# Loaded operand tiles are rounded later in the instruction lists of a one-core encoder layer

## The chip, the core and the metric

The kernel runs on one core of a Trainium2 chip. The metric is the device time of one execution in microseconds (us). Five engines work beside each other, each through its own list of instructions in order: PE multiplies matrices, DVE and ACT work on vectors, POOL does a little, and SP issues almost all transfers (DMA). An instruction that waits for another engine or for a transfer holds all that stands behind it in its list.

## What is computed

One layer of a hybrid encoder on a sequence of 2048 tokens of width 1024, all in float32:

```
xn = rms_norm(x)
[aq|ak|av|mq|mk|mv|mo|i|f|ga|gm] = xn @ w_in
A = chunked band attention (8 heads of 64; own chunk of 64 and 8 before; relative bias)
M = mLSTM matrix memory (4 heads of 128), conv on q and k, norm, sigmoid gate
y = sigmoid(ga) * (A @ w_att_proj) + sigmoid(gm) * (M @ w_mlstm_proj)
x = x + y @ w_out
x = x + relu(rms_norm(x) @ w_up)^2 @ w_down
out = rms_norm(x)
```

## The kernel before

Tokens are in four blocks of 512, two blocks to a half `s`. Large products are made with seven block products in place of eight, on sums and differences of operands; `m` numbers the seven. Each float32 operand is split into two rounded parts, a high part and the rest, and a product takes three matmuls (`mm3`, L562 to L564, and the loop of L631 and L662). A weight tile `wsp` is split by a cast on ACT (L501) and a subtract on DVE (L503). There are three `wsp` buffers, so the next split waits until PE is done with an older tile.

The other operand is kept in one of 28 tiles `r`, each of two parts. Some operands are made in one stage, stored in DRAM in float32, and loaded later into such a tile, into its second part. `take_u1` (L2101) does that: SP issues the load (L2103), `split` (L1106) casts the tile's second part to its first part on ACT (L1109), and DVE subtracts in place (L1114). It serves three sources: `xu`, the input's combinations for the later input projection (`take_batch`, 28 tiles); `u`, the hidden layer of the feed-forward part (`take_u`, 224 tiles, in a ring of 8 tiles for the first half and 16 for the second); and `mix`, pieces of the attention and memory results (`load_mix`). The down product (`down`, L806) goes through `m` and four chunks `c`, takes four `u` tiles for each, and gives them back to the ring. During the first half's down product PE also does attention and memory work for blocks 2 and 3; during the later input projection it does that for blocks 0 and 1.

The order of the instructions is found by a planner, `Flow`, when the program is built. Each step is a Python generator that yields its engine, the time that it is reckoned to keep the engine, and, for a load, the further time until it has landed. `Flow.run` always takes the step that can start first by these times, and writes its instructions down. These times are no waits: on the chip, only semaphores make an engine wait. They decide where an instruction stands in its engine's list. The tool that builds the program may move instructions a little after that; an instruction on DVE is bound not to pass one that the planner puts over 10 us earlier, on ACT over 6 us earlier.

Names that recur: L1674 adds parts of the memory's result on DVE; L1262 is the product of attention weights and values on PE; L1273 copies a bank on ACT and L1275 adds on DVE behind it; L1116 and L1765 on DVE prepare the operand `y`.

Of the kernel before, what the change touches and what calls it, by code (L numbers as in the profile page):

```python
# [101 lines left out]
class Flow:  # L102
# [12 lines left out]
               sp=dict())  # L115
# [130 lines left out]


class Layer:
    LATE = 4000.0

    def __init__(self, tc, pool, psum, io):
        self.tc, self.nc, self.io = tc, tc.nc, io
# [197 lines left out]
    def split_w(self, i, src, raw, sent=None):  # L450
        if i == 0:
            yield from self.split_first(src, raw, sent)
            self.fl.put(self.wraw, raw, late=self.LATE)
            return
# [4 lines left out]
        yield from self.split_now(i, raw)  # L459
        self.fl.put(self.wraw, raw, late=self.LATE)  # L460

    def split_turned(self, i, srcs, raw):
# [3 lines left out]
        yield from self.split_now(i, raw)  # L466
        self.fl.put(self.wraw, raw, late=self.LATE)

# [38 lines left out]
    def quad_w(self, i, q, kept, raws, evs):  # L507
# [10 lines left out]
        def sub(n, dst, x, y):  # L518
            yield "dve", dve_ns(1024)
            V.tensor_sub(dst, x, y)  # L520
            if kept:
                fl.spawn(keep(n, dst), 1)
            else:
                fl.set(spilt[n])
# [16 lines left out]
        yield from sub(2, b, d, b)  # L541
        fl.put(self.wraw, d, late=self.LATE)
        yield "wait", [spilt[1]]
        yield from sub(3, a, c, a)
        fl.put(self.wraw, c, late=self.LATE)
        yield from self.split_now(i + 5, b)
        yield "wait", [spilt[2]]
        fl.put(self.wraw, b, late=self.LATE)
        yield from self.split_now(i + 6, a)
# [1549 lines left out]
        fl.put(self.rpool, *(yield "get", ring, N_RING[s]))  # L2099

    def take_u1(self, src, r, ev):  # L2101
        yield "sp", 800, 2000
        self.nc.sync.dma_start(r[:, 1].bitcast(F32), src)  # L2103
        yield from self.split(r[:, 1].bitcast(F32), r)
        self.fl.set(ev)
# [458 lines left out]
```

## Time and profile before

| | before |
|---|---|
| median of 3 runs | 2750.84 us (2749.84 to 2754.76) |
| profiled execution | 2753.07 us, span 2751.3 us |
| PE busy | 2724.6 us (99%) |
| DVE busy | 2086.0 us (76%) |
| ACT busy | 1526.4 us (55%) |
| HBM | 458.79 MB read, 212.21 MB written |

The page gives busy time as a share of the span, and for groups of instructions their count, busy time, mean time of one, and the idle time of the engine just before them with what ended it. A matmul's row gives 390 ns, but matmuls overlap, so their spacing is less. All times are counted from the span's start.

### The profile page before, as it was taken

Reading aid. Unit: us, or ns where it says so; the run is one execution under the profiler, and the core shown is the slowest. Engines: PE = TensorE matmul, PEld = TensorE weight load, DVE = VectorE, ACT = ScalarE, POOL = GpSimd, SP = SyncE. Lnnn points to the kernel's source line nnn. Section 1 sums busy time; section 2 is a strip of 40 time slices with the busy share of each in tenths; the row PEclk is TensorE's granted clock in tenths of the full one; section 3 lists DMA queues with packets and bytes.
Section 4 is the critical chain, followed back from the end, with each engine's and each line's share of the span. In section 5 each row is a group of like instructions: output and inputs, shape, how many; then the busy total and the mean of one; then the engine's idle time right before and its main releaser. Section 6 shows DMA issues by size and latency. Waiting matters only on the chain.

```text
span 2751.3 us, 38074 instructions
## 1 busy us (share of the span) xinstructions
PE 2724.6 (99%) x12832; PEld 2261.5 (82%) x12832; DVE 2086.0 (76%) x3689; ACT 1526.4 (55%) x2640; POOL 44.6 (2%) x79
## 2 busy tenths in 40 slices
PE   9999999999999999999999999999999999999998
PEld 8878888788888887888888888888888888888887
DVE  7878776888775778897768889888888665667675
ACT  6545446666652434566556766657345565554443
POOL 0000000000000000000000000000000000000000
PEclk9999999999999999999999999999999999999999
DMA  8877678878877888767668778776864454588863
GB/s 295 284 254 268 234 267 281 260 235 266 255 256 254 299 305 294 244 212 260 246 237 295 254 231 223 239 257 199 294 227 171 151 205 154 180 278 281 283 230 137
DMA packets 331992, 673.57 MB, mean 245 GB/s; under 512 B 36900, under 2 KB 66468, under 8 KB 331796
## 3 DMA queue, kind: packets, MB, share of 16 engines
q1 hardware_dynamic: 331076, 670.08, 72.3%
q8 instruction: 101, 1.65, 0.2%
q10 hardware_dynamic: 720, 1.06, 0.1%
q14 instruction: 95, 0.78, 0.1%
HBM read 458.79 MB, written 212.21 MB: 244 GB/s over the span
## 4 chain that ended last, share of the span: by engine, by line
PE 83%; DVE 7%; DMA 4%; issue 3%; ACT 2%; POOL 0%; SPq 0%; POOLq 0%; DVEq 0%; ACTq 0%
PE bank L631 35%; PE bank L662 9%; PE bank L562 9%; PE bank L564 8%; PE bank L563 8%; PE bank L667 2%; PE bank L1337 2%; PE bank L1262 2%; PE bank L1369 2%; DVE wsp L503 1%; PE bank L856 1%; DVE r L1114 1%; DMA yp<-tmp 1%; DMA r<-u 1%; DVE ctx L1765 1%
## 5 line engine op out<-in xcount | busy, mean ns | idle before, releaser
L631 PE MATMUL bank<-r,wsp 128*128 128x512 f32 x4872 | 1110.9, 390 | 4.2 <-ACT r L1109 1.4
L631 PEld LDWEIGHTS bank<-r,wsp 128*128 128x128 f32 x4872 | 912.5, 188 | 198.2 <-ACT r L1109 2.1
L501 ACT CAST wsp<-wraw 128x1024 fp32r<-128x1024 f32 x439 | 461.3, 1051 | 492.1 <-PE bank L631 183.3
L503 DVE TENSOR_TENSOR wsp<-wraw,wsp 128x1024 fp32r<-128x1024 f32 x439 | 537.0, 1223 | 247.0 <-ACT wsp L501 236.7
L562 PE MATMUL bank<-r,wsp 128*128 128x512 f32 x1088 | 429.9, 396 | 0.3 <-DVE scs L1343 0.3
L564 PE MATMUL bank<-r,wsp 128*128 128x512 f32 x1088 | 425.3, 391 | 0.0
L563 PE MATMUL bank<-r,wsp 128*128 128x512 f32 x1088 | 425.2, 391 | 0.0
L662 PE MATMUL bank<-r,wsp 128*128 128x512 f32 x1512 | 370.8, 394 | 3.1 <-DVE ctx L780 2.5
L662 PEld LDWEIGHTS bank<-r,wsp 128*128 128x128 f32 x1512 | 279.4, 189 | 59.4 <-issue 2.7
L564 PEld LDWEIGHTS bank<-r,wsp 128*128 128x128 f32 x1088 | 204.3, 188 | 43.0
L562 PEld LDWEIGHTS bank<-r,wsp 128*128 128x128 f32 x1088 | 204.5, 188 | 38.4 <-DVE scs L1343 0.7
L563 PEld LDWEIGHTS bank<-r,wsp 128*128 128x128 f32 x1088 | 204.7, 188 | 38.1
L1114 DVE TENSOR_TENSOR r<-r 128x512 fp32r<-128x512 f32 x273 | 181.8, 687 | 56.8 <-ACT r L1109 55.0
L1109 ACT CAST r<-r 128x512 fp32r<-128x512 f32 x273 | 164.7, 621 | 104.4 <-DMA r<-u 77.1
L1798 DVE TENSOR_TENSOR ctx<-bank,ctx 128x512 f32<-128x512 f32 x150 | 103.0, 687 | 64.7 <-PE bank L631 63.6
L520 DVE TENSOR_TENSOR wraw<-wraw,wraw 128x1024 f32<-128x1024 f32 x112 | 136.5, 1220 | 2.2 <-DMA wsum<-wraw 1.0
L1350 ACT ACTIVATE sc<-sc,scs 128x640 f32<-128x640 f32 (+4 forms) x128 | 97.2, 760 | 54.9 <-DVE scs L1343 54.3
L1790 ACT COPY ctx<-bank 128x512 f32<-128x512 f32 x150 | 87.2, 581 | 52.0 <-PE bank L631 50.5
L2119 ACT ACTIVATE ctx<-ctx 128x512 f32<-128x512 f32 x96 | 60.5, 630 | 97.8 <-DVE ctx L1798 97.8
L1374 DVE TENSOR_TENSOR r<-bank,r 128x512 fp32r<-128x512 f32 (+1 forms) x168 | 96.4, 595 | 8.4 <-ACT r L1372 7.5
L1262 PE MATMUL bank<-r,r 128*128 128x512 f32 x336 | 95.7, 367 | 3.5 <-DVE ctx L1674 1.9
L1372 ACT CAST r<-bank 128x512 fp32r<-128x512 f32 (+1 forms) x168 | 80.7, 514 | 27.9 <-PE bank L1369 27.4
(257 smaller groups left out, 3054.1 us busy)
## 6 DMA issues: line engine op xcount, KB each, us to landing
wraw<-in_wf SPq DMA_DIRECT2D x196, 512.0 KB, 4.2
r<-u SPq DMA_DIRECT2D x224, 256.0 KB, 4.4
wraw<-wsum SPq DMA_DIRECT2D x104, 512.0 KB, 4.5
u<-ctx SPq DMA_DIRECT2D x128, 256.0 KB, 2.8
u<-tmp SPq DMA_DIRECT2D x96, 256.0 KB, 2.1
wraw<-in_w SPq DMA_DIRECT2D x47, 512.0 KB, 4.5
ctx<-in_wf SPq DMA_DIRECT2D x88, 256.0 KB, 4.2
wsum<-ctx SPq DMA_DIRECT2D x88, 256.0 KB, 3.1
```

The costliest lines, as they stand in the source:

```text
L501: nc.scalar.copy(w[:, 0], raw)
L503: nc.vector.tensor_sub(w[:, 1], raw, w[:, 0].bitcast(F32))
L520: V.tensor_sub(dst, x, y)
L562: mm(ps, lh, rh, start=first, stop=False)
L563: mm(ps, lh, rl, start=False, stop=False)
L564: mm(ps, ll, rh, start=False, stop=last)
L631: mm(ps, wv[:, x, k, n], a[:, y], start=new and k == 0 and x == y == 0, stop=k == 3 and x == 1, skip_group_check=True)
L662: mm(ps, wv[:, x, k, n], a[:, y], start=start and x == y == 0, stop=stop and x == 1, skip_group_check=True)
L1109: self.nc.scalar.copy(dst[:, 0], src)
L1114: self.nc.vector.tensor_sub(dst[:, 1], src, dst[:, 0].bitcast(F32))
L1262: nc.tensor.matmul(bkv[:, :, c0:c0 + w], st, sl[:, :, o:o + w], start=n == 0, stop=n == total - 1)
L1798: nc.vector.tensor_add(t[:, o:o + 512], ps, t[:, o:o + 512])
```

## The change

One number: the time after its issue at which the planner takes a tile loaded by `take_u1` as landed goes from 2000 to 10000 ns. The planner then lets the cast and the subtract start some 8 us later by its reckoning, and puts them further on in the lists of ACT and DVE. The load and the semaphores are as before. Where other steps fit in their place, the planner's later choices differ too.

```
 class Layer:
-    LATE = 4000.0
+    LATE, LANDED = 4000.0, 10000.0
...
     def take_u1(self, src, r, ev):
-        yield "sp", 800, 2000
+        yield "sp", 800, self.LANDED
         self.nc.sync.dma_start(r[:, 1].bitcast(F32), src)
         yield from self.split(r[:, 1].bitcast(F32), r)
         self.fl.set(ev)
```

More of the change, by code (lines that the diff above doesn't have):

```diff
@@ L248 @@
 class Layer:
-    LATE = 4000.0
+    LATE, LANDED = 4000.0, 10000.0
     def __init__(self, tc, pool, psum, io):
@@ L2101, in take_u1 @@
     def take_u1(self, src, r, ev):
-        yield "sp", 800, 2000
+        yield "sp", 800, self.LANDED
         self.nc.sync.dma_start(r[:, 1].bitcast(F32), src)
```

## The prediction

> **What bounds the kernel now.** I read the page first, for the busiest engine, then the waits of the moved line, then the windows and the chain of waits where that line holds somebody up.
>
> ```profile
> span 2751.3 us, 38074 instructions
> PE 2724.6 (99%) x12832; PEld 2261.5 (82%) x12832; DVE 2086.0 (76%) x3689; ACT 1526.4 (55%) x2640; POOL 44.6 (2%) x79
> L631 PE MATMUL bank<-r,wsp 128*128 128x512 f32 x4872 | 1110.9, 390 | 4.2 <-ACT r L1109 1.4
> L1114 DVE TENSOR_TENSOR r<-r 128x512 fp32r<-128x512 f32 x273 | 181.8, 687 | 56.8 <-ACT r L1109 55.0
> L1109 ACT CAST r<-r 128x512 fp32r<-128x512 f32 x273 | 164.7, 621 | 104.4 <-DMA r<-u 77.1
> ```
>
> PE is busy for 2724.6 of 2751.3 us, so everything that better order can win lies in 26.7 us, and the start and the end take part of that. The moved work is the last two rows: 273 casts on ACT and 273 subtracts on DVE, rounding in place a tile that a transfer has just brought. ACT waits 77.1 us at the head of its queue for such tiles from `u` alone. A wait there holds everything queued behind it, so the question is where PE feels it.
>
> ```profile
> 400.00:750.00 350.00, 344.51 (x1826) 290.12 (x1825) 273.27 (x704) 236.47 (x524) 13.11 (x25) 1.00 0.80 256
> 1450.00:1800.00 350.00, 344.97 (x1816) 289.58 (x1816) 301.38 (x746) 237.76 (x489) 13.26 (x26) 1.00 0.80 251
> 1800.00:2100.00 300.00, 300.00 (x1445) 251.53 (x1444) 245.92 (x442) 153.03 (x273) 3.98 (x6) 1.00 0.73 242
> 2430.00:2720.00 290.00, 289.89 (x1314) 240.81 (x1313) 193.66 (x262) 134.10 (x192) 3.94 (x3) 1.00 0.73 248
> ```
>
> In these windows the columns are length, then busy time of PE, its weight loads, DVE, ACT and POOL, the granted clock, DMA share and GB/s. In the last one, where the second half of the `u` tiles is read, PE idles 0.1 us: whatever ACT waits there costs nothing now, and winning it back gains nothing. The two attention stages idle 5.49 us (350 - 344.51) and 5.03 us. These are the places to gain.
>
> **The change part by part.** It adds and removes no arithmetic. It changes one number, the time after which the planner believes a loaded tile has landed, from 2000 to 10000 ns; the load stays where it was on SP, and the cast and the subtract move back in ACT's and DVE's lists. The instruction lists of the two programs show it. At the place in the chain below, the cast stands ahead of eleven ACT instructions of the recurrence and of attention in the old list and behind them in the new one; the subtract moves behind eleven DVE instructions.
>
> ```profile
> 737.90 6.37 DMA r<-xu
> 744.30 0.63 ACT r L1109
> 744.95 0.30 DVE r L1114
> 745.56 0.30 DVE ctx L1674
> 745.90 1.04 PE bank L1262 x2
> ```
>
> This is the chain of waits between 740 and 750 us, and it names the moved instructions outright: the transfer, the cast, the subtract, and then the small DVE instruction L1674 that PE wants.
>
> ```profile
> 744.30 0.62 ACT L1109 CAST r<-r 128x512 fp32r<-128x512 f32 x1 [4.46 <-DMA r<-xu]
> 744.95 0.69 DVE L1114 TENSOR_TENSOR r<-r 128x512 fp32r<-128x512 f32 x1 [2.81 <-ACT r L1109]
> 745.90 1.04 PE L1262 MATMUL bank<-r,r 128*128 128x512 f32 x2 [1.89 <-DVE ctx L1674]
> 744.00:746.00 2.00, 0.11 (x2) 0.10 (x1) 1.05 (x3) 1.68 (x4) 0.00 (x0) 1.00 0.61 192
> 746.00:748.00 2.00, 2.00 (x5) 1.53 (x6) 1.62 (x4) 1.98 (x5) 0.00 (x0) 0.53 0.27 49
> 748.00:750.00 2.00, 2.00 (x10) 1.69 (x9) 1.84 (x3) 1.69 (x5) 0.00 (x0) 0.61 0.34 119
> ```
>
> The first three rows are the engines' timelines, the others windows. ACT stands 4.46 us, DVE 2.81 us behind it, PE 1.89 us behind both. Then PE's granted clock falls to 0.53 and 0.61 for two windows of 2 us, which loses 2 x 0.47 + 2 x 0.39 = 1.72 us of full-speed work. In the new list L1674 and what feeds it go first, and the next cast comes when the tile has landed. I take both away: 1.89 + 1.72 = 3.6 us.
>
> [...] The measured rows stand next to each other, so I keep the term.
>
> A second place of the same kind is in the later attention stage.
>
> ```profile
> 1603.60 0.62 ACT L1109 CAST r<-r 128x512 fp32r<-128x512 f32 x1 [1.69 <-DMA r<-u]
> 1605.19 0.58 ACT L1273 COPY tmp<-bank 64x512 f32<-64x512 f32 x1
> 1606.46 0.69 DVE L1275 TENSOR_TENSOR tmp<-bank,tmp 64x512 f32<-64x512 f32 x1
> 1607.21 0.73 PE L1262 MATMUL bank<-r,r 128*128 128x512 f32 x2 [1.09 <-DVE tmp L1275]
> ```
>
> The copy L1273 follows the cast on ACT, DVE follows the copy, PE waits 1.09 us for DVE. ACT's wait of 1.69 us is longer than that, so without it PE should not wait: 1.1 us. I found no other wait of PE in the two stages behind a held cast of more than 0.6 us; for the rest I book no gain.
>
> Now the cost. A later subtract is nearer to the product that needs it.
>
> ```profile
> DMA to landing us min/median/max: 2.6/4.4/8.2
> L501 ACT CAST wsp<-wraw x439: 1028/1055/1094, 9.2 to 2727.7; 128x1024 fp32r<-128x1024 f32 x147
> 2009.58 1.22 DVE L503 TENSOR_TENSOR wsp<-wraw,wsp 128x1024 fp32r<-128x1024 f32 x1
> 2010.71 2.49 DVE L1116 SCALAR_TENSOR_TENSOR r<-ctx,r 128x512 fp32r<-128x512 f32 x4
> 2013.12 1.29 DVE L1765 TENSOR_TENSOR ctx<-ctx,ctx 128x512 f32<-128x512 f32 x2
> 745.25 0.30 issue
> ```
>
> The first row is for the loads L2103. Back to back, a 512-column DVE instruction takes (2013.12 - 2010.71) / 4 = 0.60 us, a 1024-column one 2010.71 - 2009.58 = 1.13 us, and a matmul 1110.9 / 4872 = 0.228 us. With these I counted, for each moved subtract, what stands in its queue behind the last PE result that the queue waits for, against the matmuls up to the product. In the old lists the closest place has 3.2 us to spare. In the new ones the closest is near the end of the first down product, beside the preparation of `y`: 31 DVE instructions of 512 columns and 5 of 1024 stand between a weight split that waits for PE and the end of the subtract, 31 x 0.60 + 5 x 1.13 = 24.25 us, with a weight cast of 1.055 us ahead and a hand-over of 0.30 us, 25.6 us; on PE stand 113 x 0.228 = 25.8 us. Two other places have some 1.3 and 1.6 us. So the cover is nearly used up at one place and thin at two. I book 0.5 us of loss for the first; bounds are 0 and, with a slowest landing (8.2 against 4.4 us), 3.8 us more. SP loses nothing that I can price: the loads of the moved tiles keep their order among themselves, and two reloads of `mix` fall away; 273 loads become 271. PE's own order changes mainly between the pieces of attention and the down products; the numbers of short matmuls that follow short ones are nearly the same (880 and 877), so I book nothing for it.
>
> Sum: 3.6 + 1.1 - 0.5 = 4.2 us less. The profiled execution took 2753.07 us (2751.3 us of span and 1.8 us around it), so it should take 2748.9 us. It lies 2.23 us above the median of the runs, 2750.84 us, so the median should be 2746.6 us, 0.15% less.
>
> **The rivals.** *More is freed.* The stages from 400 to 750 and 1450 to 1800 us hold 5.49 + 5.03 us of idle PE. If most waits there come indirectly from held queues, the reordering could empty them: with the clock 12.2 us, 2738.6 us. For it: ACT waits in both stages for these loads.
>
> ```profile
> DMA r<-xu: 10.5, 6
> DMA r<-u: 22.1, 19
> ```
>
> These are L1109's waits between 400 and 960 and between 1450 and 2060 us. Against it: most of the single waits of PE lie by none of them.
>
> *Products wait for their tiles (slower).* At the three thin places a landing that is 3.8 us late reaches PE: 3.8 + 0.5 at the first, 3.8 - 1.3 and 3.8 - 1.6 at the others, 9.0 us. Each gap is longer than the 1.89 us above and can cost a fall of the clock of 1.72 us, 5.2 us for three. Against the gain of 4.7 us that leaves 9.5 us, 2760.3 us. It decides once two of the three gaps open with the clock's fall. For it: the spare time fell from 3.2 us to about nothing, and DVE is the fuller of the two helpers. Against it: most landings are near 4.4 us, and the later position gives 8 us of the list for just that.
>
> *Nothing to see.* The move does what it says, but the wait at 745.90 us is taken over by another instruction, since DVE and ACT carry the same work. Then the median stays at 2750.8 us. Against it: both engines stood idle there, so nothing else was due. That the lists do not move can be left out, since they are seen to.
>
> **How the numbers follow.** The forecast has a chance of 0.50, more freed 0.18, products that wait 0.16, nothing to see 0.16. A measurement of this kernel can tell about 0.2%, 5.5 us, from no change. The forecast's own range is 2744 to 2749 us, that is a gain of 2 to 7 us, and it crosses that bound, since single waits of 1 us that come or go with the new order decide: I give half of it, 0.25, to either side. Faster by over 0.2%: 0.18 + 0.25 = 0.43. Within: 0.25 + 0.14 = 0.39. Slower: 0.16 + 0.02 for new waits with no gain, 0.18. The range goes from 2739 us, where more is freed, to 2755 us, the highest of the runs shown before; it leaves out the slower rival.
>
> **What would show it.** In the profile after, ACT's wait for `r<-xu` near 740 us should be gone or short, with no low clock there; ACT's total wait of 77.1 us for `r<-u` should fall to a fraction; the window from 400 to 750 us should idle some 3.5 us rather than 5.5 us; PE should stay full from 2430 to 2720 us. The forecast is wrong if PE waits for L1114 or L1109 in the down products, above all near 2020 us, or if a new low clock appears in a stage of attention.

## The result and the profile after

The changed kernel takes 2743.72 us (median of 22 runs, 2740.22 to 2752.17), the kernel before, run beside it, 2751.05 us (22 runs, 2745.63 to 2758.34). The ratio is 0.9977 with a 95% interval of 0.9969 to 0.9985, so 6.3 us less (4.1 to 8.5). The forecast was 4.2 us less.

The profiled execution took 2751.43 us (span 2749.6 us) and is among the longest of its 22. It holds an event, told below, that a second profile of the same kernel lacks. First the page's head and the groups of the moved instructions, then windows as in the prediction (length, busy PE, weight loads, DVE, ACT, POOL, granted clock, DMA share, GB/s).

```profile
span 2749.6 us, 38031 instructions
PE 2725.0 (99%) x12832; PEld 2264.0 (82%) x12832; DVE 2082.1 (76%) x3694; ACT 1520.6 (55%) x2641; POOL 45.2 (2%) x79
L1114 DVE TENSOR_TENSOR r<-r 128x512 fp32r<-128x512 f32 x271 | 179.7, 686 | 19.2 <-ACT r L1109 18.0 <-DMA u<-tmp 0.2
L1109 ACT CAST r<-r 128x512 fp32r<-128x512 f32 x271 | 157.0, 618 | 32.2 <-DMA r<-u 27.8 <-DMA r<-xu 2.7 <-DMA r<-mix 1.3
```

```profile
400.00:750.00 350.00, 344.77 (x1833) 290.31 (x1832) 273.02 (x705) 235.52 (x524) 13.09 (x26) 1.00 0.81 259
1450.00:1800.00 350.00, 348.35 (x1840) 294.39 (x1840) 298.93 (x744) 235.31 (x486) 12.88 (x27) 1.00 0.81 255
1800.00:2100.00 300.00, 300.00 (x1442) 251.22 (x1442) 251.58 (x455) 157.73 (x280) 4.72 (x5) 1.00 0.71 235
2430.00:2720.00 290.00, 287.70 (x1291) 238.91 (x1290) 188.72 (x260) 127.20 (x189) 3.02 (x3) 0.99 0.72 243
```

The edit did what it says. ACT's wait for `u` fell from 77.1 to 27.8 us, and DVE's idle time ahead of the subtract from 56.8 to 19.2 us. PE's idle time fell from 5.03 to 1.65 us (350 - 348.35) between 1450 and 1800 us, far more than the 1.1 us booked there, but only from 5.49 to 5.23 us between 400 and 750 us, where a fall of 2 us was expected. It rose from 0.1 to 2.3 us in the last window.

What is new in the second and the last of these places: the chain of waits ahead of 687 us, then the row of PE's timeline in which it ends.

```profile
676.47 5.87 DMA ctx<-mrow
682.40 0.65 POOL ctx L1549
683.07 0.02 ACT ctx L1579
683.38 1.04 ACT wsp L501
684.44 1.24 DVE wsp L503
```

```profile
686.96 2.36 PE L662 MATMUL bank<-r,wsp 128*128 128x512 f32 x9 [1.60 <-DVE r L1374]
```

And near 2567 us, by the engines' timelines and by windows of 2 us:

```profile
2565.46 0.63 ACT L2075 ACTIVATE sc<-sc 128x512 f32<-128x512 f32 x1 [3.92 <-DMA sc<-mid]
2566.12 0.69 DVE L2079 TENSOR_TENSOR sc<-sc,sc 128x512 f32<-128x512 f32 x1 [3.16 <-ACT sc L2075]
2566.87 1.87 PE L2384 MATMUL bank<-ones,sc 128*128 128x2 f32 x8 [2.30 <-DVE sc L2079]
```

```profile
2566.00:2568.00 2.00, 1.13 (x6) 1.14 (x6) 1.64 (x2) 2.00 (x4) 0.00 (x0) 0.68 0.38 112
2568.00:2570.00 2.00, 2.00 (x7) 1.73 (x8) 1.55 (x4) 0.23 (x2) 0.37 (x1) 0.50 0.69 204
2570.00:2572.00 2.00, 2.00 (x6) 1.59 (x5) 1.09 (x1) 0.88 (x1) 0.64 (x1) 0.50 1.01 372
2572.00:2574.00 2.00, 2.00 (x7) 1.52 (x7) 0.14 (x1) 0.00 (x0) 0.00 (x0) 0.61 1.01 338
```

Both are holds of the kind that the change was to cure, by loads that it does not touch: a row load (L1547) and the load of `square_kept` (L2072), still reckoned to land after 2000 ns. The second costs 2.30 us of PE and a fall of the clock, (0.32 + 0.50 + 0.50 + 0.39) x 2 us = 3.4 us of work.

### The profile page after: what moved, and what is told of

Same layout as the page of the kernel before. It is cut to its first block, busy times and chain, and to the rows that moved or that the text cites. A ratio compares the mean times of both kernels' runs of the same rounds, so it can differ in the third digit from the quotient of the medians.

```text
span 2749.6 us, 38031 instructions
## 1 busy us (share of the span) xinstructions
PE 2725.0 (99%) x12832; PEld 2264.0 (82%) x12832; DVE 2082.1 (76%) x3694; ACT 1520.6 (55%) x2641; POOL 45.2 (2%) x79
## 3 DMA queue, kind: packets, MB, share of 16 engines
q8 instruction: 101, 1.65, 0.3%
## 4 chain that ended last, share of the span: by engine, by line
PE 67%; DVE 4%; DMA 3%; ACT 1%; issue 1%; SPq 0%; POOL 0%; POOLq 0%; DVEq 0%; ACTq 0%
PE bank L631 23%; PE bank L662 9%; PE bank L562 8%; PE bank L564 8%; PE bank L563 8%; PE bank L1262 2%; PE bank L667 2%; PE bank L1337 2%; PE bank L1369 1%; PE bank L856 1%; DVE wsp L503 1%; DMA r<-u 1%; DMA sc<-x 1%; DVE r L1114 1%; DVE wraw L520 0%
## 5 line engine op out<-in xcount | busy, mean ns | idle before, releaser
L1114 DVE TENSOR_TENSOR r<-r 128x512 fp32r<-128x512 f32 x271 | 179.7, 686 | 19.2 <-ACT r L1109 18.0
L1109 ACT CAST r<-r 128x512 fp32r<-128x512 f32 x271 | 157.0, 618 | 32.2 <-DMA r<-u 27.8
```

The lines of the kernel that those rows point to most:

```text
L1109: self.nc.scalar.copy(dst[:, 0], src)
L1114: self.nc.vector.tensor_sub(dst[:, 1], src, dst[:, 0].bitcast(F32))
```

## A measure by stage

The lists differ between kernels, but at some points all have issued the same matmuls. Every trace has 12832 of them. I counted to the same places in each: the 2827th (606.54 us in the kernel before), the 5291st (1127.72), the 6021st (1296.47) and the 9555th (2009.32). The number of matmuls of each line up to these points is the same in all kernels below, except at the first point in one of them, whose A is left out. So A (606 to 1127 us, 2464 matmuls, the first attention and the later input projection), B (1296 to 2009 us, 3534 matmuls, the second attention with the first half's down product beside it) and C (2009 us to the last matmul) compare the same work. PE's timeline shows the points, here for the kernel before and for the second profile of the changed one (first column: start).

```profile
606.54 0.73 PE L1262 MATMUL bank<-r,r 128*128 128x512 f32 x2 [0.17 <-DVE r L1374]
1127.72 0.50 PE L631 MATMUL bank<-r,wsp 128*128 128x512 f32 x1 [0.41 <-DVE r L1116]
1296.47 0.73 PE L631 MATMUL bank<-r,wsp 128*128 128x512 f32 x2 [0.59 <-DVE ctx L1798]
2009.32 0.39 PE L562 MATMUL bank<-r,wsp 128*128 128x512 f32 x1
```

```profile
606.63 0.73 PE L1262 MATMUL bank<-r,r 128*128 128x512 f32 x2 [0.17 <-DVE r L1374]
1121.78 0.50 PE L631 MATMUL bank<-r,wsp 128*128 128x512 f32 x1 [0.41 <-DVE r L1116]
1291.48 0.73 PE L631 MATMUL bank<-r,wsp 128*128 128x512 f32 x2 [0.51 <-DVE ctx L1798]
1999.61 0.39 PE L562 MATMUL bank<-r,wsp 128*128 128x512 f32 x1
```

| kernel (profiled execution) | late, in ns | A | B | C | ratio to before |
|---|---|---|---|---|---|
| before | none | 521.2 | 712.9 | 734.2 | 1 |
| e1_four | 4 tiles of xu, 10000 | 518.7 | 715.6 | 734.8 | 0.9994 (0.9985 to 1.0003) |
| e2_u_first | u, first half | 518.4 | 708.8 | 736.2 | 0.9994 (0.9985 to 1.0002) |
| e3_u_second | u, second half | 519.2 | 712.1 | 734.7 | 1.0008 (0.9998 to 1.0018) |
| e4_all_but_u_second | xu, mix, u first half | 517.8 | 706.7 | 735.0 | 0.9972 (0.9960 to 0.9983) |
| changed kernel | all, 10000 | 518.1 | 708.2 | 740.5 | 0.9977 (0.9969 to 0.9985) |
| e5_after_again | all, 10000 | 515.1 | 708.1 | 734.8 | 0.9976 (0.9967 to 0.9985) |
| e6_square_late | all, and L2072 | 516.6 | 706.6 | 733.3 | 0.9960 (0.9948 to 0.9972) |
| e7_xu_mix | xu, mix | 515.3 | 713.4 | 734.5 | 0.9989 (0.9979 to 1.0000) |
| e8_6000 | all, 6000 | 519.6 | 709.2 | 734.9 | 0.9988 (0.9980 to 0.9997) |
| e9_rows_too | all, L2072, L1547 | | 708.8 | 734.6 | 0.9976 (0.9968 to 0.9985) |
| e10_square_alone | L2072 alone | 520.8 | 709.9 | 733.9 | 0.9999 (0.9990 to 1.0007) |
| e11_14000 | all, and L2072, 14000 | 516.7 | 718.3 | 736.1 | 1.0002 (0.9992 to 1.0012) |
| e12_square_u_second_early | e4 and L2072 | 517.1 | 706.9 | 741.1 | 0.9973 (0.9963 to 0.9983) |

Each row's kernel was timed beside the kernel before on the same chip (medians of before 2753.00 us for e1 to e4, 2754.73 for e5 to e8, 2754.08 for e9 to e12).

## The experiments

**Parts of the change (e1 to e4).** In all four `take_u1` gets the landing as an argument.

```
-    def take_u1(self, src, r, ev):
-        yield "sp", 800, 2000
+    def take_u1(self, src, r, ev, landed=2000):
+        yield "sp", 800, landed
...  e1: take_batch passes  self.LANDED if m == 4 else 2000
...  e2: take_u passes      self.LANDED if s == 0 else 2000
...  e3: take_u passes      self.LANDED if s == 1 else 2000
...  e4: take_batch and load_mix pass self.LANDED, take_u if s == 0
```

e1_four, the tiles that the hold at 744 us belongs to:

> Only the four tiles of xu whose cast held ACT 4.46 us near 744 us are reckoned to land 10 us after their issue; all other loads as before. My theory (the gain is mainly that hold and the fall of the clock behind it): 3.6 us less than before, no wait of PE near 745 us. Rival (the gain is spread over the u tiles of the first half's down product): within 1 us of before.

e2_u_first:

> Only the u tiles of the first half's down product are reckoned to land later; everything up to 1450 us is as before. My theory: about 1 us less than before (the wait at 1607 us), since the hold near 744 us stays. Rival (the gain sits in the later attention stage): 3 to 4 us less than before, with nearly no idle time of PE from 1450 to 1800 us.

e3_u_second:

> Only the u tiles of the second half's down product are reckoned to land later; everything up to 2400 us is as before. My theory: no gain, since PE idled 0.1 us there; 0 to 3 us more if the new wait of 2.3 us near 2567 us in the profile after, with the clock fall behind it, comes from this part. Rival (that wait has nothing to do with the change and can come in any kernel): the same as before.

e4_all_but_u_second:

> All tiles but the u tiles of the second half are reckoned to land later. My theory: as fast as the whole change or up to 3 us faster, that is 6 to 10 us less than before, since the part left out can only cost. Rival (the second half carries a part of the gain): 3 to 5 us less than before.

Measured: medians of 2752.10, 2749.79, 2756.19 and 2744.70 us against 2753.00 us. PE's timeline of e1, then that of e2 at the place of the first term with a window:

```profile
689.09 2.32 PE L662 MATMUL bank<-r,wsp 128*128 128x512 f32 x9 [1.23 <-DVE r L1374]
946.98 13.39 PE L662 MATMUL bank<-r,wsp 128*128 128x512 f32 x56 [1.62 <-DVE ctx L780]
```

```profile
747.07 0.73 PE L1262 MATMUL bank<-r,r 128*128 128x512 f32 x2 [1.63 <-DVE ctx L1674]
```

```profile
746.00:748.00 2.00, 0.94 (x4) 0.81 (x5) 1.89 (x4) 1.95 (x7) 0.00 (x0) 1.00 0.34 112
```

In e1 the wait near 745 us is gone, as foretold, but others stand at 689 and 947 us, and A is 1.2 us under the mean of the four kernels with early xu (519.9). The ratio says 1.7 us less, with an interval from 4.1 less to 0.8 more; the 3.6 us are still inside it, but the trace speaks against them: against e2 and e3, which have the hold but no low clock, A of e1 is no shorter. In e2 and e3 the list around 745 us is the old one: the wait is there with 1.63 and, at 746.48 us, 1.68 us, but the clock stays at 1.00. So the 1.72 us of low clock belong to some executions, not to all.

e2 frees B: 708.8 us, and ACT's waits for `u` between 1450 and 2060 us fall from 22.1 to 5.5 us. By its time, 1.7 us less with an interval from 4.1 less to 0.6 more, the 1 us that I expected and the 3 to 4 us of the rival cannot be told apart; B, 4 us shorter, speaks for the rival. e3 frees nothing, and its profile has no wait near 2567 us. e4, without the second half's `u`, gives all of the gain.

**The same kernel, and three next to it (e5 to e8).**

```
e6:  square_kept   -        yield "sp", 800, 2000     (L2072)
                   +        yield "sp", 800, self.LANDED
e7:  as e4, with both halves of u at 2000
e8:  -    LATE, LANDED = 4000.0, 10000.0
     +    LATE, LANDED = 4000.0, 6000.0
```

> The changed kernel itself once more, as the yardstick for the three runs beside it. Expected: 6 us under the kernel before (0.9977, as measured first), 2742 to 2744 us in most executions and some 8 us more in about one of three. If the longer executions come from the wait for L2079 near 2567 us, a profile that falls on a short execution shows no such wait and no half clock there; if they come from elsewhere, it shows it as well. Theory A (holds: a cast that stands at ACT's head for a landing tile delays what follows) and theory B (the gain comes from which pieces of attention the new list puts beside each other, not from the holds) say the same here.

> The changed kernel, and the load L2072 of square_kept (first step of the squares that end in L2079 and L2384) is reckoned with the 10000 ns landing as well. Theory A: ACT's wait of 3.92 us for sc<-mid at 2565 us goes, with it PE's wait of 2.30 us and the half clock of 6.8 us behind it (3.4 us of work): the executions 8 us above the others become rare, the median falls 0 to 2 us against the changed kernel run beside it, the highest execution by 5 us or more. Theory B: single holds say nothing; the long executions stay as frequent, the median moves by up to 3 us to either side.

> All of xu and mix reckoned at 10000 ns, u of both halves at 2000 as before. Theory A: the hold of 4.46 us for xu at 744 us goes, and the waits of 10.5 us in all for xu in the attention of the first half; the second half keeps its holds for u. Gain 2 to 4 us against the kernel before, the stage from 400 to 750 us idles 1 to 2 us less, that from 1450 to 1800 us as before (idle 5.03 us). Theory B: what the four parts give does not add up; all parts but the last u gave 8 us, the first u alone some 2 to 3, the four tiles alone about 1, so this one would have to give the missing 4 to 5 us, and could as well give none.

> The changed kernel with a reckoned landing of 6000 ns instead of 10000. The loads land 4.4 us after their issue by the median, 8.2 us at most. Theory A: most casts then come after their tile has landed: ACT's wait for u stays below 40 us (77.1 before, 27.8 at 10000), and the time is within 2 us of the changed kernel's. Theory B: another value deals another list, and the time falls anywhere from 7 us under the kernel before to 3 us over it, whatever ACT's waits are.

Measured: 2746.69, 2743.39 (five runs), 2750.93 and 2750.60 us against 2754.73 us. Windows of e5, then one of e6:

```profile
400.00:750.00 350.00, 346.15 (x1845) 291.99 (x1844) 274.58 (x707) 237.14 (x528) 12.90 (x26) 1.00 0.82 260
1450.00:1800.00 350.00, 347.80 (x1839) 293.95 (x1838) 299.97 (x744) 235.82 (x490) 12.48 (x27) 1.00 0.83 254
```

```profile
2430.00:2720.00 290.00, 290.00 (x1325) 241.41 (x1324) 189.85 (x259) 130.75 (x192) 3.84 (x3) 1.00 0.73 243
```

e5's profile, a shorter execution, has neither the wait near 2567 us nor the low clock; C is 734.8 us rather than 740.5. Its ratio is the first one again, but its executions do not fall into two groups 8 us apart, as was expected; they spread from 2743.16 to 2751.45 us. In e6 the wait for `sc<-mid` is gone, PE is full from 2430 to 2720 us, and the highest of its runs is 2745.66 us against 2751.45 us in e5, as theory A said, though five runs against eleven show little of the rare long ones; its median lies 3.3 us lower, more than the 0 to 2 us said. e7 frees A (515.3) and leaves B as before (713.4), which was theory A's forecast; with e2, which frees B alone, the two ratios add up to 4.7 us, and e4, which has both, gives 7.7 us (4.7 to 11.0). e8 is a miss for theory A: the time is 3.9 us above e5's, not within 2, and ACT's wait for `u` is not below 40 us.

```profile
ACT r L1109 <- DMA r<-u: 63.5, 56, 3.6
```

So a tile that lands 4.4 us after its issue by the median is still met too early in a list that reckons with 6 us. A is that of the old lists, with the wait at 746.57 us (1.66 us), and B has two thirds of the gain.

**Further in the same direction (e9 to e12).**

```
e9:   as e6, and L1546 (row load)  yield "sp", 800, self.LANDED
e10:  the kernel before with the edit of e6 in L2072 alone
e11:  as e6, with LANDED = 14000.0
e12:  as e4, with the edit of e6 in L2072
```

> As the run with L2072 reckoned late (0.9960 of the kernel before), and the row load L1547 (ctx<-mrow, which POOL L1549 and then ACT L1579 wait for) is reckoned at 10000 ns too. Theory A: PE's wait for L1374 near 686 us (1.39 to 1.60 us where it was large, its chain starts at that load) goes; 0 to 2 us less than with L2072 alone, 0.9955 to 0.9960. Theory B: the list of the first attention is dealt anew from about 545 us on, other waits come, and the time moves by up to 4 us to either side of 0.9960.

> The kernel before with L2072 alone reckoned at 10000 ns, xu, u and mix at 2000. Theory A: ACT's waits for sc<-x near 2200 to 2228 us go, and PE's wait of 0.48 us at 2231 us that hangs on them; waits for sc<-mid and sc<-fin go too, but before shows no PE wait there. Gain 0.5 to 3 us (the same edit on the changed kernel gave about 4). Theory B: what it gave there was a lucky list; here it gives nothing or a loss of up to 3 us.

> The changed kernel with L2072 late, all landings reckoned at 14000 ns instead of 10000. Theory A: 6000 ns gave half the gain and left 63.5 us of ACT's waits for u, 10000 left 28 to 39 us, so 14000 leaves under 20 us; the time is 0 to 2 us less than with 10000 (0.9952 to 0.9960), unless a product now waits for a subtract, which would show as PE waits for L1114 and give 2 to 5 us back. Theory B: anything from 0.9955 to 0.999.

> xu, mix, the first half's u and L2072 at 10000 ns, the second half's u at 2000. It tells what the second half's u is worth. Theory A: PE shows no wait behind those casts in 2430 to 2720 us in the kernel before, so the part is worth nothing: 0.9960 within 1 us, as with the second half's u late too. Theory C: the second half's u put late is a loss by itself (0.8 in 1000 when done alone), so this is 2 us better, 0.9952.

Measured: 2748.03, 2753.65, 2755.88 and 2747.57 us against 2754.08 us. e11 first: ACT's waits for `u`, windows, and PE's timeline in the first down product.

```profile
ACT r L1109 <- DMA r<-u: 24.4, 24, 2.8
```

```profile
1450.00:1800.00 350.00, 343.68 (x1821) 287.72 (x1820) 296.77 (x759) 243.69 (x509) 14.04 (x29) 1.00 0.81 249
1800.00:2100.00 300.00, 295.27 (x1402) 246.12 (x1401) 240.54 (x414) 142.57 (x245) 2.12 (x3) 1.00 0.72 237
```

```profile
2026.86 1.20 PE L562 MATMUL bank<-r,wsp 128*128 128x512 f32 x4 [1.47 <-ACT r L1109]
2029.02 0.50 PE L563 MATMUL bank<-r,wsp 128*128 128x512 f32 x1 [0.97 <-DVE r L1114]
```

ACT waits less for tiles than with 10000 ns, but now PE waits for their casts and subtracts: 1.47 and 0.97 us near 2027 us, and 0.91 us at 1531, 0.18 at 1551, 1.23 at 1915 and 0.58 at 1928 us, 5.3 us in all directly behind L1109 or L1114. The kernel before has no such wait after 1450 us. B is 718.3 us, 11 us more than with 10000, C some 2 us more, and the whole gain is gone. This is the prediction's slower rival, at a higher value of the same number. Theory A had the gain grow a little and named this loss as what could spoil it, with 2 to 5 us; it is 11.6 us against e6 by the ratios.

In e9 the chain that began at the row load is gone, but the first attention was dealt a new list with waits of its own (1.35 us for `qfar` at 461 us, 1.09 us at 492 us), two down products wait for L1114 (0.24 and 0.43 us), and it is slower than e6. e10 is 0.3 us less, with an interval from 2.8 less to 1.9 more: C is 0.3 us shorter, no more, and the old list has no wait of PE near 2567 us to lose; theory A's 0.5 to 3 us are not seen, though the interval does not rule them out. e12 shows what the second half's late `u` may be good for; ACT's timeline, then PE's:

```profile
2679.69 0.62 ACT L1109 CAST r<-r 128x512 fp32r<-128x512 f32 x1 [5.92 <-DMA r<-u]
```

```profile
2682.74 1.11 PE L2260 MATMUL bank<-const,ctx 128*128 128x128 f32 x4 [4.12 <-DVE ctx L2183]
```

A `u` tile met early holds ACT for 5.92 us, and PE stands 4.12 us behind L2183, with half clock for 6.8 us after it. Whether it is more than this one profile (C 741.1 us) stays open: e12 and e6 differ by 0.0013 in ratios from two chips, and their intervals meet. Theory C's 2 us of gain are not seen.

## Why the prediction was right, step by step

**The bound and the second half.** PE idled 0.1 us from 2430 to 2720 us, and putting those tiles late was said to gain nothing. C is 734.7 us in e3 and 734.2 before; right, for the lists as they stood there. That such a list can also have a hold there, 2567 us in the changed kernel and 2683 us in e12, was not in the sum; the sign named for this window, that PE stays full, failed in the first profile (2.30 us idle) and held in e5 (0.30 us).

**The first term, 3.6 us at 744 us.** The hold, its wait and the low clock are gone in both profiles of the changed kernel. The size of A's gain agrees: 519.9 us is the mean with early xu (before, e2, e3, e10), 516.7 the mean with late xu (the changed kernel, e4, e5, e6, e7, e12), 3.2 us, and the two groups do not overlap (518.4 to 521.2, 515.1 to 518.1). But the way there was not the one booked. Without that one hold A is only 1.2 us shorter (e1): other waits took its place, as the rival "nothing to see" had it. And the low clock was there in only two of the five profiles that have the wait (before and e10, not e2, e3 and e8). What is left is for the other 24 tiles of `xu` and for `mix`; e7 moves just these and the four, and has the whole gain of A. So it is luck that 3.2 us came out so near to 3.6 us. The sign named for it, 3.5 us of idle time from 400 to 750 us, failed in the first profile, 5.23 us, for the wait of 1.60 us at 687 us came; in e5, which has no such wait, it is 3.85 us.

**The second term, 1.1 us.** This is the step that was mis-sized. B goes from 712.8 us (mean of before, e1, e3, e7, e10) to 707.6 us (the changed kernel, e2, e4, e5, e6, e12), 5.3 us, again without overlap (709.9 to 715.6, 706.6 to 708.8; e9, left out here, has 708.8 too). What failed is the sentence that finds no other wait of PE behind a held cast of more than 0.6 us and books no gain for the rest. These waits of the kernel before are gone in e2, which moves only the casts of this stage:

```profile
1544.80 0.62 PE L1337 MATMUL bank<-r,r 128*128 128x384 f32 x2 [0.19 <-DVE r L1374]
1560.79 0.66 PE L1651 MATMUL bank<-const,ctx 128*128 128x128 f32 x4 [0.56 <-DVE ctx L1641]
1712.08 1.09 PE L1369 MATMUL bank<-const,sc 128*128 128x128 f32 x8 [0.46 <-ACT sc L1357]
1714.30 0.40 PE L1463 MATMUL bank<-g_lf,const 128*128 128x16 f32 x2 [1.13 <-DVE g_lf L1461]
1782.07 0.73 PE L1262 MATMUL bank<-r,r 128*128 128x512 f32 x2 [0.31 <-DVE r L1374]
```

The largest of them, 1.13 us, stands behind a cast that was held for 0.58 us, so the length of a hold does not bound the wait that it leaves. The chain of waits of the kernel before that leads to it:

```profile
1705.04 7.55 DMA r<-u
1712.61 0.63 ACT r L1109
1713.26 0.69 DVE r L1114
1713.95 0.09 DVE g_p L1457
1714.07 0.19 DVE g_lf L1461
```

Three more stand behind moved instructions whose tiles had landed: the subtracts keep DVE busy ahead of the step that PE wants, four of them in a row (2.49 us from 1541.34 us) ahead of the first wait, one each ahead of the second (1559.44 us) and the last (1779.46 us). So an early cast and subtract cost in two ways, by holding a queue and by taking their own time ahead of more urgent steps. For the wait at 1712.08 us I found no moved instruction in front. ACT lost 22.1 us in 19 waits in this stage, and PE met the lateness at other lines. That half of the rival "more is freed" was right.

Of the 5.3 us, 3.0 us are idle time of PE in B (means of the two groups 4.63 and 1.66 us). The rest lies where the prediction booked nothing, since their number stays the same: in the short matmuls, those of attention and memory, that follow short ones. From start to start, idle time left out, they take 121.0 to 122.1 us in B with the first half's `u` early and 118.5 to 119.4 us with it late. The difference sits in pairs that stand over 0.06 us further apart than the median of their kind, 47 to 55 of them early and 29 to 37 late. They look like waits too short to show as idle time, since a matmul's row (390 ns) is longer than its spacing (228 ns); that reading is argued, not shown.

**The cost, 0.5 us at the first down product.** None: in the changed kernel the window from 1800 to 2100 us is full, and PE has no wait there. The place was right: it is one of those that open at 14000 ns, by 1.47 and 0.97 us. With 10000 the cover just holds (in e9, another list with 10000, it opens by 0.24 and 0.43 us), with 14000 it does not.

**The sum.** 3.2 + 5.3 = 8.5 us would have been right by the stages; 6.3 us (4.1 to 8.5) were measured. That the 4.2 us forecast lie inside this interval owes something to luck: of the three terms one agreed in size by another way, one was five times too small and one was not there. What takes the difference, if there is one, is not settled. A candidate is the event at 2567 us, 2.30 + 3.4 = 5.7 us in the profile that has it; that e6, which puts off its load, gains 0.0016 more speaks for it, but the intervals of e5 and e6 meet and the profiles differ in A and B as well.

Of the two theories, theory A explains where the time went: stage A is shorter in every profile with all of `xu` and `mix` at 10000 ns, stage B in every profile with the first half's `u` at 10000 ns, each by itself. Stage C is not shorter with the second half's `u` late. Theory A does not foretell the last two or three us of a new list; e9 and e12 came out some 3 to 6 us above what it said, as theory B allows. e6 is the fastest kernel found, at 2743.39 us against 2754.73 us.

## What to carry to other kernels

In a queue that runs in order, the believed landing time of a load is a tuning number with an optimum: too small and an early cast holds the queue (ACT for 4.46 us at 744 us in the kernel before), too large and the product waits for the cast (PE for 1.47 us near 2027 us in e11); here 6000 ns kept half of the gain, 10000 all, and 14000, with L2072 late as well, none. Price early work by the whole lateness that it leaves in a stage, in held queues and in the time that it takes itself, not by the one PE wait that stands next to the held instruction. And compare stages between points where the same matmuls have been issued; idle time in fixed windows showed 2.8 us (5.03 before, 2.20 in e5) of a gain of 5.3 in stage B.

## What the runs showed of the hardware that was not expected

The clock falls to half for 3.4 us (the kernel before: (0.47 + 0.39) x 2 us / 0.5) or 6.8 us (the changed kernel: 1.71 x 2 us / 0.5), and the length of PE's wait does not decide it alone. Waits of 1.89 (the kernel before), 2.06 (e10, at 750.48 us), 2.30 (the changed kernel) and 4.12 us (e12) were followed by a fall; waits of 1.63 (e2), 1.66 (e8) and 1.68 us (e3) at the same instruction as the first two were not, and neither was one of 2.32 us in the kernel before:

```profile
1058.25 0.94 PE L662 MATMUL bank<-r,wsp 128*128 128x512 f32 x3 [2.32 <-DVE ctx L780]
```

The windows of the kernel before show half clock behind the wait of 1.89 us and full clock around the wait of 2.32 us (length, busy PE, weight loads, DVE, ACT, POOL, granted clock, DMA share, GB/s):

```profile
746.13:749.54 3.41, 3.41 (x10) 2.63 (x10) 2.87 (x6) 3.38 (x9) 0.00 (x0) 0.50 0.36 99
1056.00:1058.00 2.00, 0.00 (x0) 0.00 (x0) 2.00 (x4) 0.09 (x1) 0.00 (x0) 1.00 0.34 98
1058.00:1060.00 2.00, 1.75 (x8) 1.47 (x9) 1.97 (x5) 1.86 (x3) 0.00 (x0) 1.00 0.88 297
1060.00:1062.00 2.00, 2.00 (x10) 1.65 (x9) 2.00 (x4) 1.39 (x3) 0.00 (x0) 1.00 0.33 129
```

A shorter wait, of 0.98 us, was followed by slower matmuls in PE's timeline of e10:

```profile
31.29 1.73 PE L1068 MATMUL bank<-const,r_in 128*128 128x128 f32 x8 [0.98 <-POOL r_in L1033]
32.67 0.77 PE L562 MATMUL bank<-wsp,r 128*128 128x512 f32 x1
33.25 0.63 PE L563 MATMUL bank<-wsp,r 128*128 128x512 f32 x1
33.67 0.63 PE L564 MATMUL bank<-wsp,r 128*128 128x512 f32 x1
34.10 0.63 PE L562 MATMUL bank<-wsp,r 128*128 128x512 f32 x1
```

The last three start 0.42 to 0.43 us apart, 0.23 us once past 35.26 us. The mean clock of the first 100 us is 0.98 in e10 (as in e1) and 1.00 in the kernel before, where PE also waits 0.98 us ahead of this line, L1068, at 30.34 us. So the same wait came with a fall in one execution and without one in another; what decides it, these runs do not show.
